# A rebuilt opening: squares summed in column groups, three pairs' scales on TensorE, loads moved ahead, engines in program order

## The chip, the core and the metric

One NeuronCore of a Trainium2 chip runs the whole kernel. The metric is the device time of one execution in microseconds, the median of several runs. TensorE is PE in the rows, VectorE DVE, ScalarE ACT, GpSimd POOL and SyncE, which issues most transfers, SP.

## What is computed

One layer of a diffusion backbone: adaLN modulation, a combined input projection that feeds latent attention and a gated DeltaNet, an output projection, and a gated MLP. The change lies in the first step, the modulated RMSNorm of 256 latent and 256 context tokens of width 2048 and the first columns of the input projection:

```
sh1, sc1, g1, sh2, sc2, g2 = split(silu(c) @ w_ada + b_ada, 6)          # csh1, csc1, ... from c_ctx
h     = rmsnorm(x,   norm_mix) * (1 + sc1)  + sh1
h_ctx = rmsnorm(ctx, norm_mix) * (1 + csc1) + csh1
... = h @ w_in, h_ctx @ w_in         # 96 + 6 x 128 columns of it in the opening
```

All values are float32; a product is made of float32r matmuls of high and low parts.

## The kernel before

D = 2048 lies on partitions in 16 tiles of 128 (k = 0 to 15), the 256 tokens of each stream in the free dimension. `xl` and `xc` hold x and ctx. The opening (lines 288 to 403) does this:

- `spread` (310) makes `scb`, silu(c) and silu(c_ctx) spread over all partitions, with 32 float32 matmuls and eight copies on DVE; `scb` of the latent stream also goes to DRAM (`Sc`, 384) for a later stage.
- `Rms.add` (199) squares each tile of both streams on ACT (line 202) and adds over partitions by `col_sum` (160): for each tile 16 matmuls with one column, 256 in all, each traced as two instructions (`ss`). `Rms.finish` (211) makes the reciprocal root (`rsq` on POOL, 168) and spreads it over partitions (`row_bcast`, into `bc`).
- `shift_mm(p)` (320) makes the shifts of tiles 2p and 2p+1 on PE: it loads four `raw` tiles of w_ada (five buffers, which later weights share), multiplies 16 times by `csf` in four column groups of 32 (`amp`, 32 instructions), copies the sums on ACT (`row`), adds them with `col_sum` and adds the bias on DVE (335).
- `scale_cols(k)` (342) makes the scales of tile k on DVE: a multiply-and-sum over 2048 columns for each stream (`junk`, 347, called a dot here), then 348. Its weights `wt` have three buffers.
- `load_first(k)` (350) loads the 864 columns of w_in for tile k (`gr`, two buffers). `h_prep(k)` (355) splits them into `gh` (ACT) and `gl` (DVE, both at line 116/117 of `split`), scales x (DVE, 362), adds the shift into the high part of H (ACT, 363) and makes its low part (DVE, 364). `first_mm(k)` (367) multiplies: seven column blocks, two streams, three matmuls, 42 for a tile, all into seven PSUM banks (`fp`) that hold until k = 15.

Each engine runs its own instructions in the order of its queue. That order is not the program's: a planner arranges the instructions from estimated costs, and only what is marked by `keep_in_program_order` stays as written (PE has such a wrapper, `TensorE`, used in later stages). SP's queue is first in, first out: a load whose buffer isn't free yet holds those behind it. After the loop come the projections (`mmp`), the scans, the attention and the MLP, 1714 us in which no line is changed.

Of the kernel before, what the change touches and what calls it, by code (L numbers as in the profile page):

```python
# [8 lines left out]
F32 = mybir.dt.float32  # L9
# [7 lines left out]
P = 128  # L17
D = 2048
# [34 lines left out]
def hybrid_block(ctx: ExitStack, tc: tile.TileContext, io, dbg=None):  # L53
    nc = tc.nc
    act, dve, pool, sync = nc.scalar, nc.vector, nc.gpsimd, nc.sync

    class TensorE:

        pinned = False

        def matmul(self, *a, **k):
            i = nc.tensor.matmul(*a, **k)  # L62
            if self.pinned:
                tc.keep_in_program_order(i)
            return i

        def transpose(self, *a, **k):
            i = nc.tensor.transpose(*a, **k)
            if self.pinned:
                tc.keep_in_program_order(i)  # L70
            return i

    pe = TensorE()
# [226 lines left out]
    dve.tensor_scalar(out=b1, in0=bada[:, 16:32], scalar1=1.0, scalar2=None, op0=ALU.add)  # L300
# [6 lines left out]
    sel = pa.tile([P, 2], F32, name="sel")  # L307
    sync.dma_start(sel, io["sel"])

    def spread():  # L310
        for s in range(2):
            for q in range(4):
                bp = psm.tile([P, 4, P], F32, tag="mm", name="scp")
                for j in range(4):
                    pe.matmul(bp[:, j], sc[:, 4 * q + j, s : s + 1].broadcast_to([P, P]), ident, start=True, stop=True)
                dve.tensor_copy(scb[:, s, q * 512 : q * 512 + 512], bp.rearrange("p a b -> p (a b)"))

    Sc = dram.tile([2, P, GR], F32, name="Sc")

    def shift_mm(p):  # L320


        amp = psa.tile([P, T + 4], F32, tag="aux", name="amp")
        for m in range(4):
            raw = wr.tile([P, GR], F32, tag="raw", name="raw", bufs=NR)
            sync.dma_start(raw, io["wadab"][p, m])
            for j in range(4):
                pe.matmul(amp[32 * j : 32 * j + 32, :T], csf[:, 4 * m + j], raw[:, j * T : j * T + T], start=m == 0, stop=m == 3)
        row = pa2.tile([P, T], F32, tag="row", name="row", bufs=1)
        act.copy(row, amp[:, :T])  # L330
        for j in range(2):
            col_sum(amp[:, T + 2 * j : T + 2 * j + 2], row[:, j * P : (j + 1) * P], sel)
        for j in range(2):
            k = 2 * p + j
            dve.tensor_scalar(out=shs[:, k], in0=amp[:, T + 2 * j : T + 2 * j + 2], scalar1=bada[:, k : k + 1], scalar2=None, op0=ALU.add)

    def load_scale(k):
        w = pa2.tile([P, D], F32, tag="wt", name="wt", bufs=NW)
        sync.dma_start(w, io["wadas"][k])
        return w  # L340

    def scale_cols(k, w):

        m = pa2.tile([P, 2], F32, tag="scm", name="scm")
        for s in range(2):
            junk = pa2.tile([P, D], mybir.dt.bfloat16, tag="junk", name="junk", bufs=1)
            dve.tensor_tensor_reduce(out=junk, in0=w, in1=scb[:, s], scale=1.0, scalar=0.0, op0=ALU.mult, op1=ALU.add, accum_out=m[:, s : s + 1])  # L347
        dve.tensor_scalar(out=aas[:, k], in0=m, scalar1=b1[:, k : k + 1], scalar2=nmix[:, k : k + 1], op0=ALU.add, op1=ALU.mult)

    def load_first(k):  # L350
        gr = pa2.tile([P, G3], F32, tag="gr", name="gr", bufs=2)
        sync.dma_start(gr, io["wfirst"][k])
        return gr

    def h_prep(k, gr):

        gh = pa2.tile([P, G3], F32R, tag="gh", name="gh")
        gl = pa2.tile([P, G3], F32R, tag="gl", name="gl")
        split(gr, gh, gl)
        for s, xs in enumerate((xl, xc)):  # L360
            x, sh, aa = xs[:, k], shs[:, k, s : s + 1], aas[:, k, s : s + 1]
            dve.scalar_tensor_tensor(out=x, in0=x, scalar=aa, in1=bc[:, s], op0=ALU.mult, op1=ALU.mult)
            act.activation(H[s][:, k, 0], x, AF.Identity, bias=sh, scale=1.0)  # L363
            dve.scalar_tensor_tensor(out=H[s][:, k, 1], in0=x, scalar=sh, in1=H[s][:, k, 0], op0=ALU.add, op1=ALU.subtract)
        return gh, gl

    def first_mm(k, gh, gl):
        for j, (o, m) in enumerate(FW):
# [19 lines left out]
    shift_mm(0)  # L388
    scale_cols(0, wts.pop(0))
    wts[1] = load_scale(1)  # L390
    rms.finish(1.0 / D, bc)
    first_ps = [(psm if j < 4 else psa).tile([P, 512], F32, tag="mm" if j < 4 else "aux", name="fp") for j in range(2 * N1 + 1)]
    grs = {0: load_first(0)}
    for k in range(KD):
        hk = h_prep(k, grs.pop(k))
        if k + 1 < KD:
            if k % 2 == 0 and k + 2 < KD:
                shift_mm(k // 2 + 1)
            scale_cols(k + 1, wts.pop(k + 1))
            grs[k + 1] = load_first(k + 1)  # L400
            if k + 2 < KD:
                wts[k + 2] = load_scale(k + 2)
        first_mm(k, *hk)
# [949 lines left out]
def host(i):  # L1353
# [89 lines left out]
```

## Time and profile before

| | us |
|---|---|
| median of 3 runs (1888.59 to 1899.64) | 1891.56 |
| the profiled execution | 1896.02 |
| its span, first to last instruction | 1894.0 |
| PE busy in the span | 1807.8 (95%) |
| DVE busy | 1414.9 (75%) |
| ACT busy | 928.0 (49%) |

The profile is one execution. Its page gives busy times of the whole span; the stage of the change is read from tables of shorter stretches, from lists of waits and from the instructions in order of time. PEclk is the clock granted to TensorE, 1.00 for 2.4 GHz and 0.50 for 1.2 GHz. A matmul's listed duration reaches from its start to its end in the array, and the next one starts before that: how fast they follow is read from the starts. In the rows, `x` is the number of instructions, and a float32 matmul counts as two.

### The profile page before, as it was taken

The numbers are of one execution on the slowest core, as the hardware profiler recorded it, in microseconds if no ns is written. First come the engines' busy times: TensorE is split into PE (matmuls) and PEld (weight loads), VectorE is DVE, ScalarE is ACT, GpSimd is POOL, SyncE is SP. The second block draws the span as 40 slices with busy tenths as digits, with TensorE's granted clock in tenths as the row PEclk, the third lists the DMA queues.
The fourth block names the chain that finished last, engine by engine and source line by source line (L and its number), as shares of the span: only waits on it lengthen the run. The fifth ranks groups of instructions, "written<-read, shape, count | busy, mean of one in ns | idle before, by whom it ended". The sixth has DMA issues, their size and how long they took to land.

```text
span 1894.0 us, 33623 instructions
## 1 busy us (share of the span) xinstructions
PE 1807.8 (95%) x12674; PEld 1543.9 (82%) x12674; DVE 1414.9 (75%) x2838; ACT 928.0 (49%) x1890; POOL 44.6 (2%) x45
## 2 busy tenths in 40 slices
PE   6988999999999999898999997999999999999999
PEld 4777788888788887776888886888888888888888
DVE  4888899878877777475679876878888777755554
ACT  3223544444676656432245655555555555544443
POOL 0000001000000000000000000000000000000000
PEclk7888999999999999998999999999999999999999
DMA  8884488884787867777776775676777766666663
GB/s 297 326 310 154 129 251 245 236 229 131 227 261 235 235 215 231 260 262 251 257 272 207 229 241 150 225 234 219 232 222 216 223 186 188 180 198 203 193 198 121
DMA packets 195155, 420.26 MB, mean 222 GB/s; under 512 B 61297, under 2 KB 101361, under 8 KB 192561
## 3 DMA queue, kind: packets, MB, share of 16 engines
q1 hardware_dynamic: 168368, 403.97, 67.3%
q10 hardware_dynamic: 26624, 14.16, 2.5%
q8 instruction: 99, 1.62, 0.3%
q14 instruction: 64, 0.52, 0.1%
HBM read 389.09 MB, written 28.84 MB: 221 GB/s over the span
## 4 chain that ended last, share of the span: by engine, by line
PE 74%; issue 10%; DVE 8%; DMA 5%; ACT 2%; POOL 1%; SPq 0%; ACTq 0%; POOLq 0%; DVEq 0%
PE fps L62 25%; PE dps L62 13%; PE mmp L62 11%; PE gtp L62 8%; PE fp L62 3%; DMA rawa<-in_wada 2%; DVE junk L347 2%; PE brp L62 1%; PE op L62 1%; PE kps L62 1%; DVE wlo L117 1%; PE vps L62 1%; PE kp L62 1%; PE amp L62 1%; DMA raw<-in_wgd 1%
## 5 line engine op out<-in xcount | busy, mean ns | idle before, releaser
L117 DVE TENSOR_TENSOR wlo<-raw,whi 128x512 fp32r<-128x512 f32 (+1 forms) x940 | 634.6, 686 | 209.2 <-ACT whi L116 200.3
L116 ACT CAST whi<-raw 128x512 fp32r<-128x512 f32 (+1 forms) x940 | 576.1, 619 | 418.4 <-PE dps L62 114.4
L62 PE MATMUL fps<-H,whi 128*128 128x512 f32 x1376 | 482.6, 398 | 6.6 <-DVE H L117 6.2
L62 PE MATMUL fps<-H,wlo 128*128 128x256 f32 x1376 | 374.1, 282 | 0.5 <-DVE wlo L117 0.5
L62 PEld LDWEIGHTS fps<-H,whi 128*128 128x128 f32 x1376 | 253.9, 189 | 64.7 <-issue 4.9
L62 PEld LDWEIGHTS fps<-H,wlo 128*128 128x128 f32 x1376 | 259.2, 188 | 8.3 <-DVE wlo L117 0.9
L62 PE MATMUL gtp<-h,whi 128*128 128x512 f32 x640 | 239.8, 409 | 7.8 <-ACT whi L116 7.8
L62 PE MATMUL mmp<-h,whi 128*128 128x512 f32 x640 | 228.8, 400 | 0.0
L62 PE MATMUL dps<-GB,whi 128*128 128x512 f32 x560 | 195.9, 391 | 0.0
L268 DVE CUSTOM_DVE_ANT_0 rawa<-rawa,sch 128x1024 f32<-128x1024 f32 x128 | 156.0, 1221 | 46.8 <-DMA rawa<-in_wada 45.2
L62 PE MATMUL gtp<-h,wlo 128*128 128x256 f32 x640 | 178.5, 289 | 0.5 <-DVE wlo L117 0.5
L62 PE MATMUL mmp<-h,wlo 128*128 128x256 f32 x640 | 176.4, 282 | 0.0
L62 PE MATMUL dps<-GB,wlo 128*128 128x256 f32 x560 | 155.1, 282 | 0.0
L62 PEld LDWEIGHTS gtp<-h,whi 128*128 128x128 f32 x640 | 123.6, 194 | 33.8 <-ACT whi L116 8.0
L62 PEld LDWEIGHTS mmp<-h,whi 128*128 128x128 f32 x640 | 119.0, 188 | 26.0 <-ACT dkx L421 0.3
L62 PEld LDWEIGHTS gtp<-h,wlo 128*128 128x128 f32 x640 | 124.3, 194 | 6.4 <-DVE wlo L117 1.2
L62 PEld LDWEIGHTS dps<-GB,whi 128*128 128x128 f32 x560 | 105.1, 188 | 21.9
L62 PEld LDWEIGHTS mmp<-h,wlo 128*128 128x128 f32 x640 | 120.3, 188 | 3.2 <-issue 1.0
L62 PE MATMUL fp<-h,gh 128*128 128x256 f32 (+1 forms) x448 | 97.7, 313 | 17.4 <-ACT h L363 13.8
L62 PEld LDWEIGHTS dps<-GB,wlo 128*128 128x128 f32 x560 | 105.7, 189 | 0.6
L62 PEld LDWEIGHTS fp<-h,gh 128*128 128x128 f32 (+1 forms) x448 | 78.7, 210 | 30.4 <-ACT h L363 16.9
L347 DVE CUSTOM_DVE_ANT_0 junk<-wt,scb 128x2048 bf16<-128x2048 f32 x32 | 73.1, 2285 | 0.1
(547 smaller groups left out, 2619.8 us busy)
## 6 DMA issues: line engine op xcount, KB each, us to landing
rawa<-in_wada SPq DMA_DIRECT2D x128, 512.0 KB, 4.8
raw<-in_wgate SPq DMA_DIRECT2D x82, 512.0 KB, 4.3
raw<-in_wval SPq DMA_DIRECT2D x82, 512.0 KB, 4.5
raw<-in_wdown SPq DMA_DIRECT2D x80, 512.0 KB, 4.1
wt<-in_wadas SPq DMA_DIRECT2D x16, 1024.0 KB, 6.7
raw<-in_wadab SPq DMA_DIRECT2D x32, 512.0 KB, 7.0
raw<-in_wgm SPq DMA_DIRECT2D x32, 512.0 KB, 4.7
raw<-in_wgd SPq DMA_DIRECT2D x32, 512.0 KB, 5.1
```

The costliest lines, as they stand in the source:

```text
L62: i = nc.tensor.matmul(*a, **k)
L116: act.copy(hi, raw)
L117: dve.tensor_tensor(out=lo, in0=raw, in1=hi, op=ALU.subtract)
L268: dve.tensor_tensor_reduce(out=w, in0=w, in1=sch, scale=1.0, scalar=0.0, op0=ALU.mult, op1=ALU.add, accum_out=parts[:, h, j : j + 1])
L347: dve.tensor_tensor_reduce(out=junk, in0=w, in1=scb[:, s], scale=1.0, scalar=0.0, op0=ALU.mult, op1=ALU.add, accum_out=m[:, s : s + 1])
```

## The change

- The squares of two tiles at a time are made by one ACT instruction of 512 columns for each stream (for ctx of k = 8, 10, 14 by DVE), and summed over partitions by one 512-column matmul for each tile into one of four column groups of a PSUM bank (`pss`); its four partial rows are added by small sums. The reciprocal root is spread by four matmuls, and the first tile reads it from PSUM.
- `mod_mm` and `mod_cols` are the former `shift_mm` in two halves. They make all shifts, and also the scales of the pairs p = 2, 5, 7 (tiles 4, 5, 10, 11, 14, 15), whose weights are laid out for it. The other ten tiles keep the dot on DVE (`scale_dot`), up to one tile ahead (`dots`). Small operations for shifts and scales go from DVE to ACT.
- Shifts are loaded a pair ahead, `wt` and `gr` four tiles ahead (`gr` has three buffers now, three rows are loaded before the loop); `Sc` is written inside the loop, issued by ACT.
- PE, ACT and DVE keep the program order in the opening (`pe`, `oact`, `odve`). The junk of the dots shares two slots with the squares.

The diff, cut to its core: the wrapper class, the host's layouts and most removed lines, which stand in the functions above, are left out:

```diff
+SCP = (2, 5, 7)
...
+    pe, oact, odve = (Ordered(e) for e in (nc.tensor, nc.scalar, nc.vector))
+    oact.pinned = odve.pinned = True
     def pool_(name, bufs, side="left"):
...
+    dve.scalar_tensor_tensor(out=b1, in0=bada[:, 16:32], scalar=1.0, in1=nmix, op0=ALU.add, op1=ALU.mult)
...
     for s in range(2):
...
+    sel = pa.tile([P, 3], F32, name="sel")
...
     def spread():
...
                 for j in range(4):
...
+                (oact.copy if s else odve.tensor_copy)(scb[:, s, q * 512 : q * 512 + 512], bp.rearrange("p a b -> p (a b)"))
...
-    def shift_mm(p):
+    def load_shift(p):
+        raws = []
+        for m in range(4):
+            raws.append(wr.tile([P, GR], F32, tag="raw", name="raw", bufs=NR))
+            sync.dma_start(raws[m], io["wadab"][p, m])
+        return raws
+    def mod_mm(raws):
...
         for m in range(4):
             for j in range(4):
+                pe.matmul(amp[32 * j : 32 * j + 32, :T], csf[:, 4 * m + j], raws[m][:, j * T : j * T + T], start=m == 0, stop=m == 3)
...
+        oact.copy(row, amp[:, :T])
+        return amp, row
+    def mod_cols(p, scale, amp, row):
         for j in range(2):
+            col_sum(amp[:, T + 2 * j : T + 2 * j + 2], row[:, j * P : (j + 1) * P], sel[:, :2])
         for j in range(2):
+            k = slice(2 * p + j, 2 * p + j + 1)
+            out, mul, add = (aas, nmix[:, k], b1[:, k]) if scale else (shs, 1.0, bada[:, k])
+            oact.activation(out[:, 2 * p + j], amp[:, T + 2 * j : T + 2 * j + 2], AF.Identity, bias=add, scale=mul)
     def load_scale(k):
...
-    def scale_cols(k, w):
+    scm = {}
+    def scale_dot(k, s):
+        if s == 0:
+            scm[k] = pa2.tile([P, 2], F32, tag="scm", name="scm")
+        junk = pa2.tile([P, D], mybir.dt.bfloat16, tag="sq", name="junk")
+        odve.tensor_tensor_reduce(out=junk, in0=wts[k], in1=scb[:, s], scale=1.0, scalar=0.0, op0=ALU.mult, op1=ALU.add, accum_out=scm[k][:, s : s + 1])
+    def scale_fin(k):
+        oact.activation(aas[:, k], scm.pop(k), AF.Identity, bias=b1[:, k : k + 1], scale=nmix[:, k : k + 1])
     def load_first(k):
+        gr = pa2.tile([P, G3], F32, tag="gr", name="gr", bufs=3)
...
+    def first_hi(k):
+        g = [pa2.tile([P, G3], F32R, tag=n, name=n) for n in ("gh", "gl")]
+        oact.copy(g[0], grs[k])
+        return g
+    def h_prep(k, gh, gl):
+        if k:
+            odve.tensor_tensor(out=gl, in0=grs.pop(k), in1=gh, op=ALU.subtract)
         for s, xs in enumerate((xl, xc)):
+            odve.scalar_tensor_tensor(out=xs[:, k], in0=xs[:, k], scalar=aas[:, k, s : s + 1], in1=(bc if k else bcp)[:, s], op0=ALU.mult, op1=ALU.mult)
+        if k == 0:
+            odve.tensor_tensor(out=gl, in0=grs.pop(k), in1=gh, op=ALU.subtract)
+        for s, xs in enumerate((xl, xc)):
+            oact.activation(H[s][:, k, 0], xs[:, k], AF.Identity, bias=shs[:, k, s : s + 1], scale=1.0)
+        for s, xs in enumerate((xl, xc)):
+            odve.scalar_tensor_tensor(out=H[s][:, k, 1], in0=xs[:, k], scalar=shs[:, k, s : s + 1], in1=H[s][:, k, 0], op0=ALU.add, op1=ALU.subtract)
+    def first_mm(k, gh, gl, a, b):
+        for j, (o, m) in list(enumerate(FW))[a:b]:
...
             for s in range(2):
...
+    shift = load_shift(0)
+    grs = {}
+    for k in range(3):
+        grs[k] = load_first(k)
+        if k < 2:
+            wts[k + 1] = load_scale(k + 1)
+    pe.pinned = True
...
-    sync.dma_start(Sc.rearrange("h p i -> p h i"), scb[:, 0].rearrange("p (h i) -> p h i", h=2))
-    rms = Rms(pa2, KD, 2)
+    for s in range(2):
+        scale_dot(0, s)
+    pss = psa.tile([P, 512], F32, tag="aux", name="pss")
+    for k in range(0, KD, 2):
+        sq = pa2.tile([P, 2, 2, T], F32, tag="sq", name="sq")
+        oact.activation(sq[:, :, 0], xl[:, k : k + 2], AF.Square)
+        x2 = xc[:, k : k + 2]
+        if k in (8, 10, 14):
+            odve.tensor_tensor(out=sq[:, :, 1], in0=x2, in1=x2, op=ALU.mult)
+        else:
+            oact.activation(sq[:, :, 1], x2, AF.Square)
+        for j in range(2):
+            g = (k + j) % 4
+            pe.matmul(pss[32 * g : 32 * g + 32], ones.broadcast_to([P, 32]), sq[:, j].rearrange("p a b -> p (a b)"), start=k + j < 4, stop=k + j >= KD - 4)
+    part = pa2.tile([P, 512], F32, tag="sq", name="part")
+    oact.copy(part, pss)
+    msp = psa.tile([P, 4], F32, tag="aux", name="msp")
+    for n in range(4):
+        col_sum(msp[:, n : n + 1], part[:, n * P : n * P + P], sel[:, 2:3])
+    ms = pa2.tile([P, 4], F32, tag="ms", name="ms", bufs=1)
+    odve.tensor_scalar(out=ms, in0=msp, scalar1=1.0 / D, scalar2=EPS, op0=ALU.mult, op1=ALU.add)
+    rsq(pa2, ms, ms, 4)
+    scale_fin(0)
+    bc_ps = psa.tile([P, 512], F32, tag="aux", name="bc_ps")
+    for n in range(4):
+        pe.matmul(bc_ps[:, n * P : n * P + P], ms[:, n : n + 1].broadcast_to([P, P]), ident, start=True, stop=True)
+    bcp = bc_ps.rearrange("p (a b) -> p a b", a=2)
+    later = mod_mm(shift)
+    hk = first_hi(0)
+    mod_cols(0, False, *later)
+    h_prep(0, *hk)
+    oact.copy(bc, bcp)
+    shift = load_shift(1)
+    wts[3] = load_scale(3)
+    grs[3] = load_first(3)
+    first_ps = [(psm if j < 4 else psa).tile([P, 512], F32, tag="mm" if j < 4 else "aux", name="fp") for j in range(2 * N1 + 1)]
+    dots = {1: [1, 1], 2: [2, 2], 3: [3, 3], 5: [6, 6], 6: [7], 7: [7, 8], 8: [8, 9], 9: [9], 11: [12, 12], 12: [13], 13: [13]}
     for k in range(KD):
-        rms.add(xl[:, k], xc[:, k])
-    rms.finish(1.0 / D, bc)
+        p, later = (k + 2) // 2, None
+        if k > 1 and p < KD // 2:
+            if k % 2 == 0:
+                later = p, False, *mod_mm(shift)
+            elif p in SCP:
+                later = p, True, *mod_mm([wts[2 * p + m // 2][:, m % 2 * GR : m % 2 * GR + GR] for m in range(4)])
+        nxt = first_hi(k + 1) if k + 1 < KD else None
+        first_mm(k, *hk, 0, 3)
+        if k == 1:
+            later = 1, False, *mod_mm(shift)
+            first_mm(k, *hk, 3, 5)
+        if later:
+            mod_cols(*later)
+        first_mm(k, *hk, 5 if k == 1 else 3, 2 * N1 + 1)
+        for c in dots.get(k + 1, ()):
+            scale_dot(c, int(c in scm))
+        if k == 1:
+            shift = load_shift(2)
+        if k > 1 and k % 2 == 0 and k + 4 < KD:
+            shift = load_shift(k // 2 + 2)
         if k + 1 < KD:
+            if k + 1 in scm:
+                scale_fin(k + 1)
+            h_prep(k + 1, *(hk := nxt))
+        if k + 4 < KD:
+            grs[k + 4] = load_first(k + 4)
+            wts[k + 4] = load_scale(k + 4)
+        if k == 1:
+            tc.keep_in_program_order(act.dma_start(Sc.rearrange("h p i -> p h i"), scb[:, 0].rearrange("p (h i) -> p h i", h=2)))
+    pe.pinned = False
     for s in range(2):
```

## Rows read from the trace of the kernel before

**Rows 1.** Busy times of stretches; columns in the first line, (x) instructions.

```profile
core 0: us, PE busy (x) PEld busy (x) DVE busy (x) ACT busy (x) POOL busy (x), PEclk, DMA share, GB/s
...
0.00:42.24 42.24, 25.32 (x626) 20.77 (x626) 15.91 (x36) 14.78 (x39) 2.19 (x8) 0.74 0.83 302
...
42.24:179.70 137.46, 121.33 (x1009) 100.57 (x1010) 116.21 (x171) 33.00 (x59) 0.00 (x0) 0.83 0.75 275
...
179.70:1894.00 1714.30, 1661.16 (x11040) 1422.53 (x11039) 1282.75 (x2632) 880.25 (x1792) 42.45 (x37) 0.99 0.69 216
```

**Rows 2.** Waits in the loop: who for whom, us in total, times, longest.

```profile
ACT h L363 <- DVE xl L362: 49.3, 9, 6.5
...
PE fp L62 <- ACT h L363: 13.8, 7, 2.8
```

**Rows 3.** PE in order of time: start, duration, what, idle before.

```profile
63.12 0.71 PE L62 MATMUL fp<-h,gh 128*96 128x256 f32 x4 [2.03 <-ACT h L363]
...
73.93 0.28 PE L62 MATMUL fp<-h,gl 128*128 128x256 f32 x1
...
77.44 0.28 PE L62 MATMUL fp<-h,gl 128*128 128x256 f32 x1
...
78.00 1.07 PE L62 MATMUL amp<-raw,csf 128*32 128x256 f32 x16
...
81.50 1.06 PE L62 MATMUL amp<-raw,csf 128*32 128x256 f32 x8
```

**Rows 4.** Single microseconds of the loop, columns as in rows 1.

```profile
64.00:65.00 1.00, 1.00 (x11) 0.59 (x3) 1.00 (x1) 0.00 (x0) 0.00 (x0) 0.75 1.00 406
...
70.00:71.00 1.00, 1.00 (x7) 1.00 (x6) 1.00 (x2) 0.00 (x0) 0.00 (x0) 0.50 0.55 121
...
71.00:72.00 1.00, 1.00 (x9) 1.00 (x9) 1.00 (x1) 0.00 (x0) 0.00 (x0) 0.84 0.97 362
```

**Rows 5.** Chain that ended last, before the loop: start, duration, what.

```profile
4.15 10.12 PE scp L62 x64
...
17.16 4.47 issue
...
24.39 3.16 issue
```

**Rows 6.** Groups before the loop: operation, count, busy us, mean ns, idle.

```profile
L202 ACT ACTIVATE sq<-xl 128x256 f32<-128x256 f32 x16 | 6.4, 409 | 19.1 <-PE ss L62 13.8 <-DMA xl<-in_xT 5.3
...
L168 POOL TENSOR_TENSOR ms<-ms,half 128x4 f32<-128x4 f32 x1 | 1.0, 1022 | 33.8 <-DVE ms L214 33.8
...
L219 ACT COPY bc<-bc_ps 128x512 f32<-128x512 f32 x1 | 0.6, 586 | 4.9 <-PE bc_ps L62 4.9
```

**Rows 7.** Groups of the loop, columns as in rows 6.

```profile
L347 DVE CUSTOM_DVE_ANT_0 junk<-wt,scb 128x2048 bf16<-128x2048 f32 x30 | 68.5, 2285 | 0.0
...
L62 PE MATMUL amp<-sel,row 128*32 128x2 f32 x112 | 2.4, 186 | 0.0
...
L348 DVE TENSOR_SCALAR aas<-scm,b,vecs 128x2 f32<-128x2 f32 x15 | 4.3, 285 | 0.3
...
L117 DVE TENSOR_TENSOR gl<-gr,gh 128x864 fp32r<-128x864 f32 x16 | 16.9, 1054 | 4.9 <-ACT gh L116 4.9
...
L362 DVE SCALAR_TENSOR_TENSOR xl<-xl,aas,bc 128x256 f32<-128x256 f32 x15 | 7.2, 482 | 0.2
```

**Rows 8.** SP's own wait up to the loop's end, columns as in rows 2.

```profile
SPq L352 <- DVE gl L117: 66.2, 14, 9.7
```

**Rows 9.** Transfers up to the loop's end: count, KB each, time to landing.

```profile
wt<-in_wadas SPq DMA_DIRECT2D x16, 1024.0 KB, 6.7
...
raw<-in_wadab SPq DMA_DIRECT2D x32, 512.0 KB, 7.0
...
gr<-in_wfirst SPq DMA_DIRECT2D x16, 432.0 KB, 3.8
```

**Rows 10.** Busy times of 20 to 30 us, columns as in rows 1.

```profile
20.00:30.00 10.00, 4.93 (x245) 4.56 (x249) 0.00 (x0) 4.77 (x15) 0.00 (x0) 0.50 1.00 409
```

More of the change, by code (lines that the diff above doesn't have):

```diff
@@ L55, in hybrid_block, with __init__, __getattr__, issue @@
     act, dve, pool, sync = nc.scalar, nc.vector, nc.gpsimd, nc.sync
[L57 to L73, printed above, removed]
+    class Ordered:
+        def __init__(self, engine):
+            self.engine, self.pinned = engine, False
+        def __getattr__(self, name):
+            f = getattr(self.engine, name)
+            def issue(*a, **k):
+                i = f(*a, **k)
+                if self.pinned:
+                    tc.keep_in_program_order(i)
+                return i
+            return issue
+    pe, oact, odve = (Ordered(e) for e in (nc.tensor, nc.scalar, nc.vector))
+    oact.pinned = odve.pinned = True
     def pool_(name, bufs, side="left"):
@@ L299, in hybrid_block @@
     dve.tensor_scalar(out=sc, in0=sc, scalar1=0.5, scalar2=None, op0=ALU.mult)
-    dve.tensor_scalar(out=b1, in0=bada[:, 16:32], scalar1=1.0, scalar2=None, op0=ALU.add)
+    dve.scalar_tensor_tensor(out=b1, in0=bada[:, 16:32], scalar=1.0, in1=nmix, op0=ALU.add, op1=ALU.mult)
     csf = pa.tile([P, KD, 32], F32, name="csf")
@@ L306, in hybrid_block @@
         dve.tensor_copy(csf[:, :, s], sc[:, :, s])
-    sel = pa.tile([P, 2], F32, name="sel")
+    sel = pa.tile([P, 3], F32, name="sel")
     sync.dma_start(sel, io["sel"])
@@ L340, in load_scale @@
         return w
-    def scale_cols(k, w):
[L344 to L348, printed above, removed]
+    scm = {}
@@ L350, in load_first @@
+    def scale_dot(k, s):
[5 more added lines that the diff above has]
+        oact.activation(aas[:, k], scm.pop(k), AF.Identity, bias=b1[:, k : k + 1], scale=nmix[:, k : k + 1])
     def load_first(k):
-        gr = pa2.tile([P, G3], F32, tag="gr", name="gr", bufs=2)
+        gr = pa2.tile([P, G3], F32, tag="gr", name="gr", bufs=3)
@@ L352, in load_first @@
         sync.dma_start(gr, io["wfirst"][k])
         return gr
[L355 to L359, printed above, removed]
-        for s, xs in enumerate((xl, xc)):
[L361 to L365, printed above, removed]
@@ L367, in first_mm @@
-    def first_mm(k, gh, gl):
-        for j, (o, m) in enumerate(FW):
+    def first_hi(k):
[5 more added lines that the diff above has]
+            odve.tensor_tensor(out=gl, in0=grs.pop(k), in1=gh, op=ALU.subtract)
+        for s, xs in enumerate((xl, xc)):
+            odve.scalar_tensor_tensor(out=xs[:, k], in0=xs[:, k], scalar=aas[:, k, s : s + 1], in1=(bc if k else bcp)[:, s], op0=ALU.mult, op1=ALU.mult)
[5 more added lines that the diff above has]
+            odve.scalar_tensor_tensor(out=H[s][:, k, 1], in0=xs[:, k], scalar=shs[:, k, s : s + 1], in1=H[s][:, k, 0], op0=ALU.add, op1=ALU.subtract)
@@ L382, in hybrid_block @@
         sync.dma_start(xc[:, ks], io["ctxT"][:, ks])
-    spread()
-    sync.dma_start(Sc.rearrange("h p i -> p h i"), scb[:, 0].rearrange("p (h i) -> p h i", h=2))
-    rms = Rms(pa2, KD, 2)
-    for k in range(KD):
-        rms.add(xl[:, k], xc[:, k])
-    shift_mm(0)
-    scale_cols(0, wts.pop(0))
-    wts[1] = load_scale(1)
-    rms.finish(1.0 / D, bc)
-    first_ps = [(psm if j < 4 else psa).tile([P, 512], F32, tag="mm" if j < 4 else "aux", name="fp") for j in range(2 * N1 + 1)]
-    grs = {0: load_first(0)}
@@ L394, in hybrid_block @@
-    for k in range(KD):
-        hk = h_prep(k, grs.pop(k))
-        if k + 1 < KD:
[L397 to L403, printed above, removed]
+    shift = load_shift(0)
[4 more added lines that the diff above has]
+            wts[k + 1] = load_scale(k + 1)
@@ L1368, in host @@
     wa = i["w_ada"][0]
-    a["sel"] = np.ascontiguousarray((np.arange(P)[:, None] % 32 == np.arange(2)[None]).astype(np.float32))
+    q = np.arange(P)[:, None]
+    a["sel"] = np.ascontiguousarray(np.concatenate([q % 32 == np.arange(2)[None], q % 32 == 0], 1).astype(np.float32))
     a["wadab"] = np.ascontiguousarray(wa[:, :D].reshape(4, 4, P, 8, T).transpose(3, 0, 2, 1, 4)).reshape(8, 4, P, 1024)
-    a["wadas"] = np.ascontiguousarray(wa[:, D : 2 * D].T).reshape(KD, P, D)
+    a["wadas"] = np.ascontiguousarray(wa[:, D : 2 * D].T).reshape(KD, P, D).copy()
+    nat = wa[:, D : 2 * D].reshape(2, 2, 4, P, 8, T).transpose(4, 0, 3, 1, 2, 5).reshape(8, 2, P, D)
+    for p in SCP:
+        a["wadas"][2 * p : 2 * p + 2] = nat[p]
     wi = i["w_in"][0]
```

8 lines of the change are left out of this document (removed).

## Prediction

> **What bounds the kernel now.** I read the busy table of stretches first, to see which part of the span the change can reach. The opening and the loop over the 16 tiles of D take 179.7 of 1894.0 us; the other 1714.3 us run at a granted clock of 0.99 with TensorE (PE) busy for 1661 us, and no line of the change lies there [rows 1]. In the loop (42.24 to 179.70, 137.5 us) PE is busy 121.3 us and VectorE (DVE) 116.2 us, each with idle time between, at a clock of 0.83 and with DMA moving 275 GB/s, so no engine alone is the bound [rows 1]. The waits say what is: ScalarE (ACT) waits 49.3 us for the DVE's xl before it can write h, and PE waits 13.8 us, seven times and up to 2.8 us, for that h [rows 2]. It is a chain from DVE over ACT to PE, once per tile. The gaps cost twice: PE stood still for 2.03 us up to 63.12 [rows 3], and after it the clock was 0.75 in the microsecond from 64, 0.50 in that from 70 and on its way back in that from 71 [rows 4]. From 64.5 to 71.3 PE ran at 1.2 instead of 2.4 GHz, half of which, 3.4 us, is lost besides the gap itself.
>
> How fast PE could be is read where it streams. Between two gl matmuls at 73.93 and 77.44 lie 30 matmuls of first_mm: 0.117 us each at the full clock. A block of eight amp instructions takes 1.07/2 = 0.53 us at the full clock and 1.06 us at the half one [rows 3].
>
> **The part before the loop.** Now the first matmul of the loop starts at 42.24. The broadcast of sc (spread) ends at 4.15 + 10.12 = 14.3 and stays; behind it PE stands still twice, 4.47 and 3.16 us, put down to "issue", while it works through 512 one-column ss instructions [rows 5]. The change replaces these 512 by 32 (16 matmuls of 512 columns in column groups) and 32 for the small sums. Step by step, in the order that the change fixes:
> - ACT now copies the second half of scb: the last copy ends at 14.3 + 0.6 = 14.9 (0.59 us for 512 columns [rows 6]). Then DVE's second dot for tile 0 runs, 14.9 to 17.2 at 2.29 us [rows 7].
> - Squares and the dots' junk now share two slots, so the second pair of tiles can be squared only from 17.2. A square of 512 columns costs between 0.41 (256 columns) and 0.59 (a copy of 512) [rows 6]; I take 0.6. Of the seven pairs left four need two on ACT and three need one (the other is on DVE): 11 x 0.6 = 6.6, that is 23.8. The matmuls follow: the four amp matmuls of 256 columns in a block cost 0.53 to 1.06, so two of 512 columns cost about the same [rows 3], less than ACT's 1.2 per pair. Last sum at 25.
> - Behind it, in series: copy 0.6, small sums 0.6, 1/D and EPS 0.2, the power on POOL 1.02 [rows 6], bc_ps by 8 instructions at 10.12/64 = 0.16 [rows 5], 1.3, and the semaphores between: 28.9.
> - Then PE does the 32 amp instructions of pair 0, 2.1 us at full and 4.2 at half clock [rows 3], ACT the row copy (0.4), PE the column sums (0.34 [rows 7]), ACT the shifts and H (1 us): first_mm can start at about 35, not at 42.24. The ends are 32 (no semaphore time, full clock) and 42 (the two issue stalls stay as they are, 7.6 us; I take them away because PE has some 190 instructions ahead of the loop where it had 626 [rows 1]).
>
> The Trainium skill, "ScalarE: Activation LUTs", section "Rules for kernel authors", puts an ACTIVATE at about 0.3 us plus 0.83 ns per element, 0.73 us for a square of 512 columns by my estimate. By it the start would be some 1.5 us later. The rows have 0.41 us where the rule gives 0.51, so I keep the rows.
>
> **The loop, engine by engine.** PE: 16 x 42 matmuls x 0.117 = 78.6 us. One block of 32 amp instructions and its column sums cost 4 x 0.53 + 0.34 = 2.5 us [rows 3, 7]; there are ten in the loop, seven for shifts as now and three new ones for the scales of tiles 4, 5, 10, 11, 14, 15: 25. Sum 103.6 us at the full clock, 4.9 us for a tile without a block and 7.4 with one.
>
> DVE: of 32 dots 20 remain, 18 of them in the loop, where 30 are now: 12 x 2.285 = 27.4 us off [rows 7]. The 32 small operations for scales and shifts (0.285 us for one [rows 7]) go to ACT, whose busy time in the loop is only 33 of 137.5 us [rows 1]. A tile costs DVE 1.0 (gl) + 4 x 0.48 + the wait for ACT's h, 2.9 us in all, and 2.3 for each dot: 7.5 with two dots, 5.2 with one. Tiles prepared during the bodies k = 0, 1, 2, 4, 6, 7 and 10 have two dots ahead of them. Of these 1, 2, 4, 6 and 10 have a block on PE (7.4 us), k = 7 is covered by the block that body 8 begins with, and k = 0 by a PE that is still at the half clock. So DVE is no longer behind PE, but only just: I leave 3 us for waits, in k = 0, 1 and 7.
>
> ACT in program order: the copy of row, gh, the two small ones, then h. PE's column sums now come after 18 matmuls (2.1 us), which hide the row copy of 0.4; after that h needs 0.3 + 0.5 + 0.5, and some 1.9 us of the body are left to hide it. If one link of this came later, PE would stand still there: that is the rival below.
>
> DMA: the loads are moved ahead in SP's queue (three rows of wfirst, three of the scale weights, pair 0 of the shifts behind x; then four tiles, or a pair, ahead). What SP may issue hangs on free slots: now its wfirst loads wait 66.2 us for gl [rows 8]. To the loop's end 16 x 1024 + 32 x 512 + 16 x 432 KB must come [rows 9], and by the code 2 x 2048 KB for x and ctx, 44.8 MB in all; at the 409 GB/s of the stretch 20 to 30 [rows 10] that is 110 us. The last of it is needed when body 13 begins, 17.2 us of PE (7.4 + 2 x 4.9) ahead of the end: the end can't lie before 2.5 + 110 + 17.2 = 130. This is 17 us under the sum below, so DMA is covered as long as it runs at over some 350 GB/s.
>
> The Trainium skill's "DMA: Bandwidth & Descriptors", section "Where 436 GB/s comes from", says that HBM gives one core about 358 GB/s. By this the bound would be 2.5 + 125 + 17 = 145, level with the forecast, and DMA would rule with PE. The trace doesn't agree, with 409 GB/s over 10 us [rows 10]; by the rule the DMA rival's chance would be 0.4.
>
> **The sum.** Start 35 + PE 103.6 + 3.4 for the half clock after the gap ahead of the first tile [rows 4] + waits 3 + the clock lost after one of them 1.7 = 146.7. The loop ends at 179.7 now, so 33 us go. The rest of the kernel is bound by PE and begins 33 us sooner; its first weights are read while the loop runs, as now. The profiled execution took 1896.0 us; 1896.0 - 33 = 1863. It lies 4.5 us above the median of the three runs, 1891.6, so the median comes to 1858.5; I say 1859. Ends of this case: start 32 and no wait, 138.9, saves 41: 1851; start 42 and twice the waits, 158.4, saves 21: 1870.
>
> **The rivals.** *DMA becomes the bound.* For it: 275 GB/s now [rows 1], the slots that SP waits for remain, and the same bytes must come in 112 us instead of 145. Against it: the loads stand earlier in the queue. At 320 GB/s on the mean, between 275 and 409: 2.5 + 140 + 17 = 160, saves 20, 1872. Chance 0.2.
>
> *The strict order opens gaps: slower.* Today a planner lets an engine pull another operation forward; a fixed order can't. If PE stands still some 2 us in a body because h comes late through ACT's queue (gh, row, shifts, scale, h), it pays 2.0 us and 3.4 for the clock [rows 4], 5.4 us a body. At six bodies the gain is gone, at eight the kernel is slower; with twelve of fifteen it is 65 - 33 = 32 us, 1923. Against it: the chain has 1.9 us of slack in the bodies with a block. Chance 0.05.
>
> *It gains little, since the time comes back later.* If the first projections behind the loop wait for weights, whose five raw slots the last shift block holds until body 12, or DVE's other work piles up there, the gain is cut to within 9 us: 1887. Against it: the last shift block is done in body 12, three bodies or 17 us ahead, and 5 x 512 KB take 6.4 us at 409 GB/s; then PE is the bound for another 1700 us [rows 1]. Chance 0.06.
>
> **How the numbers follow.** The forecast has 0.69, DMA 0.2, little change 0.06, slower 0.05. The time is the forecast's, 1859. The range takes in the forecast's own (1851 to 1870) and most of the DMA case, which reaches 1878 at 305 GB/s: 1849 to 1878. Half a per cent, 9.5 us, is what a measurement of this kernel tells from no change; faster by more 0.89, within 0.06, slower 0.05.
>
> **What would show it.** The profile after should have the first fp matmul at 32 to 38 with no long issue gap ahead; the loop's last fp at 139 to 158; a granted clock above 0.93 in the loop (now 0.83); DVE's junk at 20; DMA near 350 GB/s there; and the rest within a few us of 1714. It is wrong if the loop's clock stays near 0.83, if PE's waits name raw or wt transfers (DMA), or if the stretch behind the loop grows by what the loop gave.

## The result and the profile after

The changed kernel takes 1870.95 us (median of four runs, 1864.65 to 1875.89) where the kernel before takes 1890.34 (median of four: the three runs of the table above and one more): a ratio of 0.9872, 95% interval 0.9844 to 0.9901. Timed a second time beside other runs it came to 1870.96 and 0.9871. That is faster by 1.3%, some 19 us by the medians and 24 by the ratio; 1859 was forecast.

The profiled execution, the longest of the four, took 1875.9 us with a span of 1874.0, 20.0 less than before. The busy table of stretches (start and end; length; busy us and instructions of each engine; granted clock; DMA share; GB/s) answers to [rows 1]:

```profile
0.00:34.00 34.00, 22.42 (x184) 13.13 (x184) 12.93 (x26) 13.98 (x27) 2.19 (x8) 0.95 0.94 365
34.00:151.60 117.60, 109.82 (x1153) 94.48 (x1154) 85.77 (x120) 41.65 (x93) 0.00 (x0) 0.97 0.85 323
151.60:1874.00 1722.40, 1666.49 (x11041) 1425.93 (x11039) 1281.21 (x2632) 879.42 (x1792) 42.46 (x37) 0.98 0.69 215
```

The loop begins 8.2 us sooner (34.0 instead of 42.2) and is 19.9 us shorter (117.6 instead of 137.5), at a clock of 0.97 instead of 0.83. So it ends 28.1 us sooner. The rest, of which no line was changed, is 8.1 us longer in this execution, and 20 are left.

The waits of the loop (who waits for whom: us in total, times, longest) answer to [rows 2]:

```profile
ACT h L68 <- DVE xl L68: 23.6, 15, 5.8
DVE junk L68 <- DMA wt<-in_wadas: 8.7, 2, 6.9
DVE xl L68 <- ACT aas L68: 5.4, 7, 1.0
PE fp L68 <- ACT h L68: 5.3, 3, 3.8
PE amp L68 <- DMA raw<-in_wadab: 2.8, 4, 1.1
```

PE's wait for h fell from 13.8 to 5.3 us. A new line stands beside it: VectorE waits for a scale weight (wt), once for 6.9 us. What this one wait does is seen in order of time, first on VectorE, then on PE (start, duration, what, idle before):

```profile
73.09 2.29 DVE L68 CUSTOM_DVE_ANT_0 junk<-wt,scb 128x2048 bf16<-128x2048 f32 x1 [6.88 <-DMA wt<-in_wadas]
...
75.31 2.29 DVE L68 CUSTOM_DVE_ANT_0 junk<-wt,scb 128x2048 bf16<-128x2048 f32 x1
...
77.52 1.05 DVE L68 TENSOR_TENSOR gl<-gr,gh 128x864 fp32r<-128x864 f32 x1
78.49 0.48 DVE L68 SCALAR_TENSOR_TENSOR xl<-xl,aas,bc 128x256 f32<-128x256 f32 x1
78.89 0.48 DVE L68 SCALAR_TENSOR_TENSOR xc<-xc,aas,bc 128x256 f32<-128x256 f32 x1
```

```profile
79.56 1.05 PE L68 MATMUL fp<-h,gh 128*96 128x256 f32 x2 [3.79 <-ACT h L68]
```

The two dots are those of tile 6, while gl and the scaled x behind them are tile 5's (`dots` has `5: [6, 6]`). So the late weight was not one that tile 5 needs: the fixed order put the next tile's dots ahead of it. PE stood still for 3.79 us until 79.56, and then ran at the lower clock for some three microseconds (columns as in the first table):

```profile
80.00:81.00 1.00, 1.00 (x5) 0.91 (x5) 1.00 (x3) 1.00 (x2) 0.00 (x0) 0.50 0.96 368
81.00:82.00 1.00, 1.00 (x7) 1.00 (x6) 1.00 (x1) 0.01 (x1) 0.00 (x0) 0.50 1.11 430
82.00:83.00 1.00, 1.00 (x7) 1.00 (x7) 1.00 (x3) 0.00 (x0) 0.00 (x0) 0.54 1.05 430
83.00:84.00 1.00, 1.00 (x10) 1.00 (x10) 1.00 (x3) 0.00 (x0) 0.00 (x0) 1.00 0.94 393
```

Why that wt came late stands in SyncE's own queue. First its timeline (start, duration, queue, what), then its longest waits in the loop, which answer to [rows 8]; between them the one transfer of ScalarE's queue:

```profile
48.18 0.47 SPq L352 DMA_DIRECT2D wt<-in_wadas  x1
48.74 14.86 SPq L327 DMA_DIRECT2D raw<-in_wadab  x4
63.65 0.42 SPq L369 DMA_DIRECT2D gr<-in_wfirst  x1
64.12 0.42 SPq L352 DMA_DIRECT2D wt<-in_wadas  x1
```

```profile
49.74 0.38 ACTq L483 DMA_DIRECT2D Sc<-scb  x1
```

```profile
SPq L369 <- DVE gl L68: 47.2, 11, 8.0
...
SPq L327 <- DMA Sc<-scb: 12.7, 1, 12.7
```

Four loads of a shift pair took 14.9 us to issue, since one of them waited 12.7 us for the write of Sc to DRAM, which ScalarE had issued at 49.74. The load reads nothing of Sc, and it is in another queue. The link is in the program: the completion of each transfer is counted on one of eight semaphores, handed out in turn, and a transfer isn't issued until the one before it on the same semaphore has landed. The program of the changed kernel lists them so (the write in ScalarE's queue, and the second of the four loads):

```
L483 DMA Sc<-scb 128x2x1024 [waits DMAHW5]
...
L327 DMA raw<-in_wadab 128x1024 [waits DMAHW6,DMAHW5,PE]
```

### The profile page after: what moved, and what is told of

Read it like the earlier page. It is cut to its first block, busy times and chain, and to the rows that moved or that the text cites. A ratio compares the mean times of both kernels' runs of the same rounds, so it can differ in the third digit from the quotient of the medians.

```text
span 1874.0 us, 32978 instructions
## 1 busy us (share of the span) xinstructions
PE 1798.7 (96%) x12376; PEld 1533.5 (82%) x12376; DVE 1379.9 (74%) x2777; ACT 935.1 (50%) x1911; POOL 44.6 (2%) x45
## 4 chain that ended last, share of the span: by engine, by line
PE 72%; issue 10%; DMA 8%; DVE 6%; ACT 2%; POOL 1%; SPq 0%; ACTq 0%; POOLq 0%; DVEq 0%
PE fps L68 25%; PE dps L68 13%; PE mmp L68 11%; PE gtp L68 6%; DMA rawa<-in_wada 3%; PE fp L68 3%; PE brp L68 2%; PE op L68 1%; DVE rawa L271 1%; PE kp L68 1%; DVE wlo L120 1%; DMA wt<-in_wadas 1%; PE yp L68 1%; PE kps L68 1%; DMA raw<-in_wgd 1%
## 5 line engine op out<-in xcount | busy, mean ns | idle before, releaser
L68 PE MATMUL gtp<-h,whi 128*128 128x512 f32 x640 | 235.5, 404 | 7.0 <-ACT whi L119 7.0
L68 PE MATMUL fp<-h,gh 128*128 128x256 f32 (+1 forms) x448 | 86.3, 292 | 6.2 <-ACT h L68 5.3
L68 PEld LDWEIGHTS fp<-h,gh 128*128 128x128 f32 (+1 forms) x448 | 70.1, 191 | 12.1 <-ACT h L68 6.5
L490 ACT COPY fx<-fps 128x256 f32<-128x256 f32 x86 | 32.0, 374 | 71.6 <-PE fps L68 71.5
```

Source lines behind the costliest of these rows:

```text
L68: i = f(*a, **k)
L490: act.copy(out, ps[:M, T:])
```

## The experiments

Theory 1 (from the trace): the loop ends 5 us later than forecast since the Sc write holds SP's queue; the loads as such are covered. Its rival: the bytes bound the loop, and the wait would only move. Theory 2 (from the prediction): VectorE is "only just" not behind PE, so the dots that went to PE were needed. Its rival: that move buys nothing. Theory 3: the fixed order is a gain. Its rival: it opens gaps.

All runs in one table. "Loop" goes from the first fp matmul to the first matmul behind the loop, "rest" from there to the end, both of the profiled execution; "time" is the median of the runs, the ratio is to the kernel before in the same batch. That kernel had medians of 1890.3 to 1897.6 us in the four batches, so times of different batches are better compared by their ratios.

| kernel | loop | us | clock | DVE busy | rest | time | ratio (interval) |
|---|---|---|---|---|---|---|---|
| before | 42.2 to 179.5 | 137.3 | 0.83 | 116.2 | 1714.5 | 1890.3 | |
| changed | 34.0 to 151.5 | 117.5 | 0.97 | 85.8 | 1722.5 | 1870.95 | 0.9872 (0.9844-0.9901) |
| changed, again | 32.9 to 149.1 | 116.2 | 0.99 | 85.7 | 1725.1 | 1870.96 | 0.9871 (0.9835-0.9908) |
| Sc late | 34.0 to 147.6 | 113.6 | 0.97 | 85.5 | 1712.3 | 1863.46 | 0.9832 (0.9784-0.9880) |
| Sc late, again | 33.0 to 143.9 | 110.9 | 1.00 | 85.6 | 1710.0 | 1862.63 | 0.9820 (0.9793-0.9847) |
| Sc late, more bytes | 33.2 to 145.8 | 112.6 | 0.98 | 85.6 | 1716.7 | 1865.70 | 0.9850 (0.9808-0.9892) |
| no scales on PE | 34.1 to 151.1 | 117.0 | 0.99 | 111.0 | 1713.3 | 1869.09 | 0.9859 (0.9815-0.9902) |
| Sc late, no scales on PE | 33.2 to 149.1 | 115.9 | 0.99 | 110.9 | 1716.2 | 1867.91 | 0.9849 (0.9811-0.9886) |
| Sc late, one pair on PE | 34.1 to 146.9 | 112.8 | 0.97 | 102.3 | 1712.8 | 1866.95 | 0.9857 (0.9828-0.9885) |
| changed, planner's order | 37.4 to 158.5 | 121.1 | 0.96 | 79.6 | 1716.2 | 1881.31 | 0.9900 (0.9866-0.9935) |
| before, new squares | 34.7 to 160.6 | 125.9 | 0.89 | 115.3 | 1719.2 | 1877.49 | 0.9905 (0.9872-0.9937) |
| before, junk in two slots | 46.7 to 166.5 | 119.8 | 0.96 | 113.0 | 1714.6 | 1886.77 | 0.9952 (0.9929-0.9975) |

**The Sc write after tile 11.**

```
-        if k == 1:
+        if k == 11:
             tc.keep_in_program_order(act.dma_start(Sc..., scb[:, 0]...))
```

> The write of Sc is issued after body 11 instead of body 1. Theory: in the changed kernel the fourth load of shift pair 3 waited 12.7 us behind this write in SP's queue, the loads of tile 6 behind it came 5 us late, and PE stood still 3.8 us at 79.6 and ran at the half clock after it. Then the last fp matmul of the loop, at 151.6, comes at 145 to 148, and the whole is 3 to 6 us faster than the changed kernel (about 1866). Rival: the loop is bound by the bytes that DMA must move; then the wait moves to another tile and the loop ends at 150 to 152, the whole unchanged.

Last fp at 147.5, 1863.46 us. The four loads issue in 4.1 us, and the next wfirst row follows at 56.14 instead of 63.65 (timeline of SP's queue in this run):

```profile
48.64 4.12 SPq L327 DMA_DIRECT2D raw<-in_wadab  x4
56.14 0.33 SPq L369 DMA_DIRECT2D gr<-in_wfirst  x1
```

and of its waits in the loop

```profile
DVE junk L68 <- DMA wt<-in_wadas: 4.5, 2, 3.3
...
PE fp L68 <- ACT h L68: 3.0, 2, 1.8
```

remain of 8.7 and 5.3 us. In the loop the hold is gone, and the time with it; what waits for the write now is the load that reads it (`sch` of a later stage, line 267, for 6.8 us). So theory 1 stands as far as one execution of each kernel goes. Both kernels were therefore run once more, first the changed kernel.

> The changed kernel once more, beside the others: last fp at 150 to 153 us, one load of SP's queue held for some 12 us by the Sc write as before, a time 0.985 to 0.990 of the kernel before's, and 3 to 6 us over that of the run with the Sc write late. If its hold is absent in this execution, or the loop ends elsewhere by more than 3 us, the 12 us are a matter of the one execution and not of the program.

The hold is there again, 11.9 us (and 12.0 us in the run without scales on PE), so it belongs to the program:

```profile
SPq L327 <- DMA Sc<-scb: 11.9, 1, 11.9
```

The loop took 116.2 us. The second execution of the late write:

> The changed kernel with the Sc write after tile 11 once more, beside the run with one pair. Two things are asked. The loop: 112 to 115 us again, against 116.2 and 117.6 in the two executions with the write after tile 1. The rest of the kernel, from the last fp to the end, whose program is the same in both: 1712.3 us in the first execution with the late write, 1722.5 and 1725.1 in the two with the early one. If the rest is scatter of the execution, it is anywhere between 1712 and 1725 this time; if the early write makes it longer, it is under 1715 again. I expect 1712 to 1720.

Loop 110.9 us and clock 1.00, under what was expected; the rest 1710.0. The late write so takes 2.6 to 6.6 us off the loop (113.6 and 110.9 against 117.5 and 116.2). Off the median it takes 7 to 8 us both times, 8 to 10 by the ratios. The two kernels were never in the same batch, and the intervals of the ratios overlap at their ends; but of the ten executions with the late write nine are shorter than every one of the eight with the early one (1864.65 to 1876.14). It is the fastest version that was run.

**More bytes.** Sc late, and 12 transfers of 256 KB more.

```
             wts[k + 4] = load_scale(k + 4)
+            sync.dma_start(dram.tile([P, 512], F32, ...), io["wadas"][k, :, :512])
```

> The changed kernel with the Sc write after tile 11, and in each of tiles 0 to 11 one more transfer of 256 KB at the end of the tile's loads (the first quarter of that tile's scale weights, copied to DRAM that nothing reads). 3.1 MB more beside the 37.9 MB that the loop moves in 113.5 us. If the loop is bound by bytes, 3.1 MB at the 409 GB/s of the opening's full stretch are 7.7 us: last fp at 154 to 156 us instead of 147.5. If the loads are covered by TensorE's work, as the prediction had it: last fp at 147 to 149 us, and the whole time within 2 us of the run with the late Sc write alone. Between the two, 150 to 153: the loads come just in time, and some of them are late. I expect 148 to 151.

Last fp at 145.7, sooner than any of the cases had it and between the 147.5 and 143.8 of the two executions without the added bytes, while DMA moved 369 GB/s over the whole loop:

```profile
33.20:145.80 112.60, 107.69 (x1152) 92.81 (x1153) 85.60 (x120) 41.60 (x93) 0.00 (x0) 0.98 0.95 369
```

Against 334 and 345 without them. From 40 to 110 us it was 390 GB/s, with the DMA engines busy all the time (a share of 1.00), so there is little room for more. But these bytes are covered: the rival that DMA becomes the bound is refuted for the kernel with the late write.

**All dots on VectorE.** SCP is emptied, so that no scales come from PE, and each tile has its two dots on VectorE; once with the early Sc write, once with the late one.

```
-SCP = (2, 5, 7)
+SCP = ()
-    dots = {1: [1, 1], 2: [2, 2], 3: [3, 3], 5: [6, 6], ...}
+    dots = {k: [k, k] for k in range(1, KD)}
```

> The changed kernel with all sixteen scales as dots on DVE (two dots ahead of each tile), none on PE. Theory: DVE costs 7.5 us a tile by the trace of before and becomes the bound: the loop ends at 156 to 162, 5 to 10 us later than in the changed kernel, and PE shows 1 to 2.5 us of waiting in tiles without a shift block, with the clock lost behind them. Rival: DMA is the bound and DVE is covered; then the loop ends within 2 us of 151.6, or earlier since PE has 7.5 us less to do.

> The changed kernel with two edits together: the Sc write after tile 11 instead of tile 1, and no scales on TensorE (all dots on VectorE, two a tile). It tells what the scales of three pairs on TensorE are worth once the transfer that held back SP's queue is out of the way; with that transfer in its place, leaving them on VectorE cost nothing (last fp 151.0 us against 151.5). Theory A: TensorE and VectorE are about level in the loop (104 us of matmuls, 111 us of VectorE work in 113 us), so VectorE is the bound by little: last fp at 147 to 150 us, with the time within 0.3% of the run with the late Sc write alone (last fp 147.5, 1863 us). Theory B, that of the prediction: without the 27 us taken from VectorE the loop runs behind VectorE's dots and ends at 152 us or later, some 5 us more in the time. Theory C: TensorE's six extra pair sums (about 5 us) are the larger cost, and the loop ends earlier than 146 us.

With the early write nothing is lost, where 5 to 10 us were expected: 151.1, 1869.1 us. With the late one the loop is 115.9 against 113.6, 110.9 and 112.6 us, the time 1867.9 against 1863 to 1866. VectorE is then busy 110.9 of 115.9 us, and PE waits for h in nine small pieces:

```profile
PE fp L68 <- ACT h L68: 10.4, 9, 1.6
```

None reaches 2 us, and the clock stays at 0.99. So the move to PE was worth 2 to 5 us of the loop, and only where the Sc write didn't hide them. In the time it isn't shown: the ratios, 0.9849 against 0.9820 to 0.9850, have intervals that overlap.

**One pair on PE.** Sc late, SCP = (5,).

```
-SCP = ()
+SCP = (5,)
-    dots = {k: [k, k] for k in range(1, KD)}
+    dots = {k: [k, k] for k in range(1, KD) if k not in (10, 11)}
```

> The changed kernel with the Sc write after tile 11 and the scales of one pair (tiles 10 and 11) on TensorE instead of three. TensorE's busy time in the loop should be between that of three pairs (109.1 us) and none (103.8): some 105.6. VectorE's between 85.5 and 110.9: some 102.4. Theory A (the two engines are about level, and each waits for the other where its own share is larger): loop of 110 to 113 us, last fp at 143 to 147 us, 1 to 3 us less than with three pairs. Theory B (the loop's 113 us are TensorE's matmuls plus the loads' waits, whatever the share): 113 to 115 us, no gain. Theory C (VectorE's dots become the bound where no pair is on TensorE, tiles 1 to 9): 115 us or more, as without any pair (115.9).

Loop 112.8 us, PE busy 106.3, VectorE 102.3: within theory A's range in the loop, but no better than three pairs, and 1866.95 us. The gain that a better balance should have brought isn't there; theory B stands as well.

**The planner's order.** The changed kernel with PE, ScalarE and VectorE left to the planner (the wrappers that pin their order are taken out: oact, odve become act, dve, and pe.pinned stays False). With it the Sc write is free too; the planner issues it at 10.3 us, far ahead of the loop.

> The changed kernel with the planner's order on PE, ACT and DVE instead of the program's. Theory: the fixed order is worth something, since the planner puts dots of later tiles ahead of what the next h needs: the loop ends at 156 to 170 and the whole is 5 to 18 us slower than the changed kernel. Rival: what counts is the work taken from DVE and the earlier loads; then the loop ends at 148 to 154 and the whole is the same within 4 us.

The loop is 121.1 us and starts 3.4 us later, 1881.31 us. PE's longest wait, 3.63 us, stands behind three dots in a row on VectorE, of which the last is for a later tile (timeline of VectorE, then of PE):

```profile
82.14 2.29 DVE L68 CUSTOM_DVE_ANT_0 junk<-wt,scb 128x2048 bf16<-128x2048 f32 x1
...
84.35 2.29 DVE L68 CUSTOM_DVE_ANT_0 junk<-wt,scb 128x2048 bf16<-128x2048 f32 x1
...
86.57 0.48 DVE L68 SCALAR_TENSOR_TENSOR xl<-xl,aas,bc 128x256 f32<-128x256 f32 x1
```

```profile
87.64 1.80 PE L68 MATMUL fp<-h,gh 128*96 128x256 f32 x7 [3.63 <-ACT h L68]
```

ScalarE's gh also stands in front of an h and waits for its row of wfirst, as at 101.87, where h follows without a pause; there it cost PE no more than 0.34 us (timeline, then waits in the loop):

```profile
101.87 0.91 ACT L68 CAST gh<-gr 128x864 fp32r<-128x864 f32 x1 [3.33 <-DMA gr<-in_wfirst]
102.69 0.50 ACT L68 ACTIVATE h<-xl,shs 128x256 fp32r<-128x256 f32 x1
```

```profile
ACT gh L68 <- DMA gr<-in_wfirst: 11.3, 3, 4.0
...
PE fp L68 <- ACT h L68: 6.3, 5, 3.6
```

So the loop ends 7 us later than in the changed kernel, and it does so without the hold by the Sc write; against the late write it is 11 to 15. In the time the gain of the fixed order is some 5 us by the ratios and 10 by the medians, the intervals overlap, and two of the seven executions (1869.25, 1870.63) are as fast as the changed kernel's. A rival had the fixed order lose.

**The squares alone.** The kernel before with the new squares and sums, ScalarE's share of the scb copies, and junk in the squares' two slots; loop and planner as before.

```
-    rms = Rms(pa2, KD, 2)
-    for k in range(KD):
-        rms.add(xl[:, k], xc[:, k])
+    (squares of two tiles, sums in column groups, as in the changed kernel)
-            junk = pa2.tile(..., tag="junk", name="junk", bufs=1)
+            junk = pa2.tile(..., tag="sq", name="junk")
```

> The kernel before with the new squares and sums alone (512-column squares, column groups, four spreading matmuls, half of scb copied by ACT); the loop, its loads and the planner's order as before. Theory: the issue gaps of 4.5 and 3.2 us go, the first fp matmul comes at 34 to 37 instead of 42.2, the loop takes 135 to 140 as before, and the whole is 6 to 8 us faster than before (about 1884). Rival: the gaps belong to the time and not to the ss instructions and return elsewhere; then 0 to 3 us.

The start is 34.7, as expected. But the loop, which wasn't touched, is 125.9 us long instead of 137.3. Of what the edit contained only junk's slots reach into the loop. By the ratio, 0.9905, this part alone has most of the gain of the whole change (0.9872); the two intervals overlap.

**Junk in two slots, nothing else.**

```
-            junk = pa2.tile([P, D], mybir.dt.bfloat16, tag="junk", name="junk", bufs=1)
+            junk = pa2.tile([P, D], mybir.dt.bfloat16, tag="sq", name="junk")
```

> The kernel before with one edit: the unused product of the scale dots (junk) shares the two buffers of the squares instead of having one of its own. Nothing is computed in another way. In the run with the new squares alone the loop took 125.8 us instead of 137.3 without any edit of the loop, and this sharing was part of that run. The program that results has VectorE's two dots of a tile side by side with gl behind them in the odd tiles, as that run had, where the kernel before has a dot, gl, a dot. Theory A: this sharing is the cause: first fp as before (42.2 us), loop 124 to 128 us long, last fp at 167 to 170 us, the time 9 to 13 us under that of before. Theory B: the earlier end of the opening is the cause (the loads were further ahead when the loop began): loop 135 to 138 us, last fp at 177 to 180, the time unchanged.

The loop is 119.8 us long, 17.5 less than before. The opening is 4.5 us longer (first fp 46.7, where 42.2 was expected), so the loop's end comes 13.0 us sooner, and the time is 1886.77, 6 us less by the medians and 9 by the ratio. In the kernel before, this one line shortens the loop by nearly as much as the whole change does (20 us). In the changed kernel the order is fixed by the program; one slot wasn't run there. How the line works is seen on VectorE. The kernel before, with one slot:

```profile
70.22 2.28 DVE L347 CUSTOM_DVE_ANT_0 junk<-wt,scb 128x2048 bf16<-128x2048 f32 x1
72.43 0.08 DVE L347 DVE_READ_ACCUMULATOR2_ANT scm<- 128x1 f32 x1
74.06 1.06 DVE L117 TENSOR_TENSOR gl<-gr,gh 128x864 fp32r<-128x864 f32 x1 [1.55 <-ACT gh L116]
75.04 2.28 DVE L347 CUSTOM_DVE_ANT_0 junk<-wt,scb 128x2048 bf16<-128x2048 f32 x1
```

and the same kernel with two:

```profile
70.34 2.28 DVE L347 CUSTOM_DVE_ANT_0 junk<-wt,scb 128x2048 bf16<-128x2048 f32 x1
72.55 0.08 DVE L347 DVE_READ_ACCUMULATOR2_ANT scm<- 128x1 f32 x1
72.55 2.29 DVE L347 CUSTOM_DVE_ANT_0 junk<-wt,scb 128x2048 bf16<-128x2048 f32 x1
74.77 0.08 DVE L347 DVE_READ_ACCUMULATOR2_ANT scm<- 128x1 f32 x1
74.77 1.05 DVE L117 TENSOR_TENSOR gl<-gr,gh 128x864 fp32r<-128x864 f32 x1
```

With one slot the planner put gl between the two dots of every second tile; gl waits for ScalarE's gh, and the second dot stands behind it in the queue. With two slots the dots stand side by side and gh is there when gl comes. VectorE's waits in the loop (who for whom, us in total, times, longest), with one slot:

```profile
DVE shs L335 <- PE amp L62: 7.9, 5, 3.3
DVE gl L117 <- ACT gh L116: 4.9, 3, 1.7
...
DVE shs L335 <- ACT gh L116: 2.8, 2, 1.4
```

and with two, with PE's wait for h, which was 13.8 in [rows 2]:

```profile
PE fp L62 <- ACT h L363: 14.6, 8, 2.7
...
DVE shs L335 <- PE amp L62: 2.5, 1, 2.5
```

The waits of gl for gh are gone, and those of the shifts (`shs`) fell from 10.7 to 2.5 us. From 54.1 to 159.5 us VectorE is now busy for 104.6 of 105.4: two tiles take it 14.9 us, which is the prediction's 7.5 for a tile with two dots. So behind the order stands VectorE's load, and at 119.8 us it is the bound. PE waits for h no less than before. What it gained is clock, 0.96 for 0.83: it is busy for 105 us instead of 121. (Some 17 of the loop's 1009 PE instructions now stand ahead of the first fp.) The instructions of the two programs are the same, in another order. Why the planner chose so with one slot, and whether VectorE's late h or PE's late sums came first in this circle, isn't shown.

## Why the prediction was right and where it was wrong

The sign and the range held: 1871 lies in 1849 to 1878. The number was 12 us too low, and what made the loop short was named only in part.

**The start: right.** 34.0 for 35. Its steps too: the last sum of the squares ended at 24.8 for 25, the power on POOL at 27.3, bc_ps at 28.5 for 28.9, and the issue stalls of [rows 5] are gone. A square of 512 columns took 627 ns, above the 0.41 to 0.59 between which the prediction had it. The rule in the Trainium skill, "ScalarE: Activation LUTs", section "Rules for kernel authors", had given 0.73 us by my estimate; the measured value lies between the rows and it, nearer to the 0.6 taken.

**The loop's end: 151.5 for 146.7.** At a clock of 1.00 (Sc late, second execution) PE is busy for 106.1 us, so the sum of 103.6 was 2.5 short. For waits and the clock 3 + 3.4 + 1.7 = 8.1 us were allowed; the changed kernel has 117.5 - 106.1 = 11.4. Start -1.0, PE +2.5, waits and clock +3.3: the 4.8 us. Of the 11.4 PE stood still for 7.8, where 3 was allowed, and lost 3.6 by the lower clock, where 5.1 was. (At the loop's start the clock was 0.56, 0.50, 0.50 and 0.73 in the microseconds from 35 to 39, some 1.7 us lost for the 3.4 counted; in the second execution with the late write it did not fall there.) The runs with the late write have 4.8 to 7.5 us in place of 11.4. So the step that failed in the loop is the term for waits, and with it the one that moved the loads: the prediction counted their slots and their bytes, but not that the Sc write, which the change also moved, from SP's queue into ScalarE's, stands before a load of SP by their common semaphore. And it counted the dots ahead of a tile as work, not as a wait: the 3.79 us are tile 5 behind tile 6's late weight.

**Why the loop is shorter: half missed.** The prediction explained the 49.3 us of [rows 2] by the amount of VectorE's work and took 27 us of dots off it. The kernel before with junk in two slots has all the dots and a loop of 119.8 us. What held the loop of 137.3 us above that was VectorE's order and waits, not its load (it was busy for 116.2), and with them the clock. The load is the bound only below: with all dots the loop takes 115.9 to 119.8 us, of which VectorE is busy for 111 to 113. Moving the dots was worth 2 to 5 us on top, in runs without the Sc hold, since PE has 106 us of its own. The line of the diff that gives junk the tag of the squares was read as a matter of the opening ("squares and the dots' junk now share two slots"), and its price there was right to about 1 us (the dot ended at 16.2 for 17.2), its effect in the loop not seen.

**DMA: right in the mechanism.** Of the marks that were named, the clock in the loop (0.97), junk (2 before the loop and 18 in it) and the first and last fp came as said; DMA moved 323 GB/s, under the 350 that the sum wanted, and yet it wasn't the bound. One sign of being wrong did show, in small: PE waited for raw, four times and for 2.8 us in all. The rival would have put the time at 1872, and 1871 came, but not by its mechanism: 3.1 MB more cost nothing at 369 GB/s. The Trainium skill's "DMA: Bandwidth & Descriptors", section "Where 436 GB/s comes from", has some 358 GB/s from HBM for one core; the trace of that run doesn't agree, with 390 over the 70 us from 40 to 110.

**The fixed order: the rival was wrong on the whole**, and its gain was at nothing in the sum: 7 us of the loop's end, as far as one execution with the planner's order shows it. In one place the rival was right: the 3.79 us are a gap of the fixed order. The chain through ScalarE had less slack than counted (a shift took 0.26 us there and a scale 0.35 to 0.39, where the rows of VectorE had 0.285 for a scale), but VectorE's waits for the scales in the profile after, seven of at most 1.0 us, cost PE little.

**The rest of the kernel: not as forecast.** "Within a few us of 1714" became 1722.5 and 1725.1. In the other executions it is 1710.0 to 1719.2. The changed kernel and the one with the late write have the same instructions in the same order on every engine except for that one write, and the early write is in the run without scales on PE too, whose rest is 1713.3. So neither the rest's program nor the write explains it. The excess lies between 460 and 890 us, where the clock differs by the execution: 0.92 in 750 to 900 of the kernel before, 0.91 and 0.86 in the same stage (some 720 to 880) of the two executions of the changed one, 0.95 with the late write. The 0.91 is too near to the 0.92 to explain it. Both profiled executions of the changed kernel are the longest of their four (1875.89 and 1876.14, the others 1864.65 to 1871.76), so part of it is the execution. The cause stays open. Of the 12.9 us by which the profiled execution (1875.9) missed its forecast of 1863, these are 8.1 and the loop the other 4.8. The range held since it was wide enough for both misses.

## What to carry to other kernels

A wait in a chain of engines can be an order, not a load: before work is moved to another engine, look whether an instruction that waits stands ahead of one that could run, and whether a single buffer of a result that nobody reads has put it there. Then look at the load again, since it is the next bound. Work of the next tile that is done ahead makes this tile wait for the next one's loads. A transfer that nobody waits for soon can still hold loads of another queue, so put it where the queue has time. And a gain of the loop's end in one profile is not yet a gain in the median: here 28 us became 19.

## What the runs showed of the hardware

- A write of 1 MB to DRAM took 12.2 us from issue to landing, while the loads of 1 MB in the same loop took 7.8 on the median, and one load of another queue was held 11.9 to 12.7 us by it (three executions).
- Nine waits of at most 1.6 us left the clock at 1.00 (Sc late, no scales on PE; the mean of 0.99 comes from the loop's start), whereas after one of 3.79 us it was at 0.50 for some three microseconds. Between these the length of a wait doesn't tell: after waits of 1.77 to 1.82 us the clock fell to 0.50 (five times in the kernel before), and after six of 1.66 to 1.83 us it stayed at 1.00 (the same kernel with two slots).
- DMA moved 390 GB/s over 70 us, from 40 to 110, with its engines busy all the time, and PE was busy for 67.9 of them (Sc late, more bytes).
